# A hybrid attention encoder block: the product over wo's sums moved by two steps, and the switch of the output lag by eight

## The chip, the cores and the metric

The kernel runs on one core of one Trainium2 chip. A core has a tensor engine (PE, with its weight loads shown apart as PEld), a vector engine (DVE), a scalar engine (ACT), a GpSimd engine (POOL) and a sync engine (SP), which here issues all transfers. [...] The metric is device time in microseconds (us); lower is better.

## The reference

One encoder layer over x (1024 tokens, 1024 features, float32):

```python
h = einsum('bsd,de->bse', x, w_in)             # 21 blocks of 128 columns, and the values
q_a, k_a, v_a, z_a, q_b, k_b, v_b, z_b = split(h)
y_a = neighborhood_attention(q_a, k_a, v_a, rel_bias)     # 8 heads, 8x16 window on a 16x64 grid
y_b = windowed_gqa_with_sink(rotary(q_b), rotary(k_b), v_b, sink)   # 8 query heads, 2 key heads, |i-j| <= 128
mixed = concat([y_a * silu(z_a), y_b * silu(z_b)])
y = einsum('bse,ed->bsd', mixed, w_out)
x = layer_norm(alpha * x + y, gain, bias)
```

## The kernel before, in words

Every float32 operand of a product is split into two float16 tiles, a high and a low part, and each product becomes three 16-bit products (high by high, high by low, low by high) that add up in one PSUM bank. For that, weights are brought to a common power of two. For the output weights wo the power comes from sums of magnitudes: 16 blocks of wo are loaded and summed on ACT (L1025) or DVE (L1027) into the 16 columns of `wom`, and `wo_scale` (L796 to L805) makes the factors of them:

```python
ps = bank("t")
nc.tensor.matmul(ps[:, :16], ones, wom.bitcast(BF16)[:, 1::2], start=True, stop=True)   # L798
# L799 to L804: six DVE instructions on one column each, to wog, wos, wsn and yc
```

**Steps and units.** The attention is 128 units, first 64 of group b (SWA), then 64 of group a (NA): for each pair of heads p, each half j, eight blocks. The main loop goes through steps; step i issues unit i's scores (`stage_qk`, two matmuls, L890 and L891, into one of four PSUM banks "s", and a DVE instruction L904 that adds the bias and finds the row's extreme) and its exponential on ACT (L920). Unit i-1 is split in the same step (ACT L938, DVE L939) and handed to a transposing transfer that SP issues (L941). The bank of unit n is free for unit n+4 when L939 of unit n is done.

**Rounds and the lag.** Four units make a round q. Its product with the values (`stage_pv`, L967) takes one of two PSUM banks "t"; a step later DVE divides by the row sums (`stage_on`, L976 and L983), which frees that bank. Every second finished round of the right kind is turned back on PE (`stage_ot`, four transposes, L1005) into a "t" bank, and DVE multiplies it into z: in group b by four instructions L992, two in the round's first step and one each in the third and fourth, in group a by one instruction L1011. `stage_ot(q-1)` and `stage_pv(q)` stand in the first step of round q, and round and place in the round come from the step number:

```python
q, m = divmod(i - LP - 3 - (i < LATE), 4)      # L1502, LP = LPP = 6
```

So round q starts at step 4q + 10 while i < LATE, and at step 4q + 9 from then on. LATE is 4*22 + 6 + 7 = 101. Group b's even rounds have transposes; in group a it is rounds 4p + 19 and 4p + 20 (19 and 20, 23 and 24, 27 and 28).

**What fills PE.** Between the scores, a generator hands out the matmuls of 15 projections (L444, 48 each), so many to each step, and at the end of the loop the first products with wo (L1239). The rest of the output projection (a Strassen-like scheme over wo's blocks, with tiles T, m, A, wo) and the layer norm follow in `final`.

**The planner.** Work that is not tied to a step (splits of weights, sums of wo's blocks) is queued by engine with a priority, dependences on earlier pieces and a cost. At each step the planner books an engine's assumed time (`due`) against the assumed time of the step (`at_step`) and issues queued pieces where it finds room (`pop`, `fill_in`). All this happens while the program is written: on the chip the order is fixed. `t_prep(i)` queues, for one block row of wo: four differences (L1072, "any" engine), four high parts on ACT (L1077), four low parts (POOL L1065 and L1066, or DVE L1063) and four stores to DRAM by SP (L1080). They need `wsn`, so `t_prep` is called right behind `wo_scale`, together with four loads of the second block row (L1019), which wait for the low parts of the first.

**Where wo_scale stands.** At the top of a step, ahead of the step's scores and of `stage_ot` and `stage_pv`, under this condition:

```python
if i >= T_GO and i % 4 == 0 and len(scans) == 16 and all(op.step is not None and op.fin + 3 < at_step(i) for op in scans):
```

T_GO is 24. It holds first at step 44, the third step of round 8.

Of the kernel before, what the change touches and what calls it, by code (L numbers as in the profile page):

```python
# [27 lines left out]
LTT, LPP, BH, ND, NA, NX, F1 = 1, 6, 9, 1, 1, 8, 0.2  # L28
# [24 lines left out]
T_GO = 24  # L53
POOL_Q, DVE_ADD, DVE_OWN = 2, range(112, 124), 1.1
M2_AT, M3_AT = 113, 122
LATE = 4 * 22 + LPP + 7
WORK = {"act": 0.55, "dve": 0.63, "pool": 1.2}
STEP = (1.88, 1.5, 1.2)
ROOM = {"act": 0.35, "dve": 0.5, "pool": 0.0}
# [7 lines left out]
def hybrid_block(ctx, tc, xT, x, wt, wv, wo, bias, sink, gain, lbias, cos, sin, bmask, out):  # L67
# [116 lines left out]
    def at_step(i):  # L184
        return STEP[0] * i - (STEP[0] - STEP[1]) * max(0, i - 121) - (STEP[1] - STEP[2]) * max(0, i - 128)
# [610 lines left out]
    def wo_scale():  # L796
        ps = bank("t")
        nc.tensor.matmul(ps[:, :16], ones, wom.bitcast(BF16)[:, 1::2], start=True, stop=True)  # L798
        nc.vector.tensor_reduce(wog, ps[:, :16], axis=mybir.AxisListType.X, op=ALU.max)  # L799
        nc.vector.tensor_scalar_max(wog, wog, 2.0 ** -30)  # L800
        nc.vector.tensor_scalar(wog.bitcast(I32), wog.bitcast(I32), 0x7F800000, None, op0=ALU.bitwise_and)
        nc.vector.tensor_scalar(wos.bitcast(I32), wog.bitcast(I32), 0x7F800000, None, op0=ALU.bitwise_xor)
        nc.vector.tensor_scalar_mul(wsn, wos, 0.25)
        nc.vector.tensor_scalar(yc, wog, mc, 4.0, op0=ALU.mult, op1=ALU.mult)  # L804
        book("dve", 0.9)  # L805
# [6 lines left out]
    def gather_v(p):  # L812
        t = va[p] = big_ap([128, 8, 4 * VE], F16, f"va{p}")
        bulk["last"] = bulk["step"]
        nc.sync.dma_start(t, vd[p].rearrange("(k c) r e -> (c r) k e", k=8))
# [40 lines left out]
    def stage_load(u, i):  # L856
        g, p, j, t = u
        if g == "a" and t == 0:
            bulk["last"] = clock["step"] + 1
            bt = big_ap([128, BWIN[3]], F32, "bias")  # L860
            nc.sync.dma_start(bt, bias[2 * p + j])
            ld = Op("sp", None, [], 1)
            ld.step = i
            op = enq("pool", lambda: nc.gpsimd.tensor_scalar(bt, bt, rsg, -1.0, op0=ALU.mult, op1=ALU.mult),
                     ld, prio=0)
            st["bias", p, j] = bt, op
# [77 lines left out]
    def quad(q):  # L944
        g, p, j, t = units[4 * q]
        return g, p, j, t // 4
# [38 lines left out]
    def stage_z(n):  # L985
        for _ in range(n if st.get("z") else 0):
            ps, k, h, e, m = st["z"].pop(0)
            o = ps.rearrange("p (b h c) -> p b h c", h=2, c=64)
            r = slice(64 * e, 64 * e + 64)
            z = zt[k][r, 512 * h:512 * h + 512].rearrange("p (b m c) -> p b m c", m=2, c=64)[:, :, m]  # L990
            book("dve", 0.42)
            nc.vector.scalar_tensor_tensor(z, o[64 * m:64 * m + 64, :, e], z_col(k)[r], z, op0=ALU.mult, op1=ALU.mult)  # L992
# [23 lines left out]
    scans = []  # L1016

    def wo_load(i, b, *deps):
        load_ops["wor", i, b] = enq("sp", lambda: nc.sync.dma_start(wor[:, b], wo[i, :, b]), *deps)  # L1019

    def wo_scan(i, b):
        def scan(eng):
            m = wom[:, 4 * i + b:4 * i + b + 1]
            if eng == "act":
                nc.scalar.activation(junk2, wor[:, b], AF.Abs, accum_out=m)  # L1025
            else:
                nc.vector.tensor_reduce(m, wor[:, b], axis=mybir.AxisListType.X, op=ALU.add, apply_absolute_value=True)  # L1027

        scans.append(enq("any", scan, load_ops["wor", i, b], prio=1.9,
                         cost={"act": 0.85, "dve": 0.68} if (clock["step"] or 0) > 4 else {"act": 0.85}))  # L1030
# [62 lines left out]
    def t_soon(n):  # L1093
        def load():
            t = big_tile(f"T{n}", (128, 2, 2, 512), F16)
            nc.sync.dma_start(t.rearrange("p i h c -> p i (h c)"), td[:2, :, n].rearrange("i p c -> p i c"))
            pair_of(t, *[(("T1", "T3", "T4", "T2")[n], i) for i in range(2)])

        load_ops["T", n] = enq("sp", load, *t_ops)
# [3 lines left out]
    def x_soon(t):  # L1103
        def load():
            xr_[t] = big_tile(f"xr{t}", (128, D), F32)
            nc.sync.dma_start(xr_[t], x[t])

        enq("sp", load)

    def b_load(n, *deps):  # L1110
        key, i = B_KEYS[n]
        b = ("B11", "B12", "B21", "B22").index(key)

        def load():
            b_raw[n] = wp.tile([128, 512], F32, tag="wr", name=f"wob{n}", bufs=5)
            nc.sync.dma_start(b_raw[n], wo[i, :, b])

        load_ops["wo", n] = enq("sp", load, *deps)
# [325 lines left out]
    for i in range(-LD, NU + LO):  # L1444
        if 0 <= i + LD < NU:
            stage_load(units[i + LD], i)
        if i < 0:
            continue
        clock["step"] = i
        per, h = divmod(i, 16)  # L1450
        bulk["step"] = i
        if (i - LP - 3 - (i < LATE)) % 4 > 1:
            stage_z(1)
        if i == VA_AT:
            gather_v(0)
        if i in SCAN_LD:
            n, b = divmod(NSCAN + SCAN_LD.index(i), 4)
            wo_load(SCAN[n], b, *scans[-4:-3])
            wo_scan(SCAN[n], b)
        if i >= T_GO and i % 4 == 0 and len(scans) == 16 and all(op.step is not None and op.fin + 3 < at_step(i) for op in scans):  # L1460
            wo_scale()
            scans.clear()
            t_prep(0)
            for b in range(4):
                wo_load(1, b, t_low[(0, 1, 3, 2)[b]])
            t_prep(1)
        if i in B_LD:
            n = B_LD.index(i)
            b_load(n, w_ops[NL - 5 + n] if n < 5 else b_ops[n - 5])
        if i in B_AT:  # L1470
            b_split(B_AT.index(i))
        if i in M_AT:
            m_queue(M_AT.index(i))
        if i == M2_AT:
            m_kq(2, ("A11", "A12", "A21", "A22"))
        if i == M3_AT:
            m_kq(3, ("A11", "A21"))
        if i == 129:
            t_soon(0)
            x_soon(0)  # L1480
            t_soon(3)
            x_soon(4)
            x_soon(1)
            t_soon(1)
            t_soon(2)
        if bulk["last"] == i:
            sp_at.append(i)
        if i >= 118:
            pop("sp", 3)
        elif sum(j > i - 3 for j in sp_at) < 2:  # L1490
            kept = len(queues["sp"])
            pop("sp", 1)
            if len(queues["sp"]) < kept:
                sp_at.append(i)
        if i < NU:
            u = units[i]
            if u[0] == "b" and u[3] == 0:
                need(*[o for j in range(2) for o in stk_ops[f"b{u[1]}", j, u[2]]])
            if u[0] == "a" and u[3] == 0:
                need(*stk_ops[u[1], u[2], 0], *stk_ops[u[1], u[2], 1])  # L1500
            stage_qk(u)
        q, m = divmod(i - LP - 3 - (i < LATE), 4)  # L1502
        if i >= Q30 + 2:
            q, m = (NU // 4 - 2, i - Q30 - 2) if i < Q30 + 4 else divmod(i - LP - 3, 4)
        elif i >= Q30:
            q, m = -1, 0
        if m == 0 and 0 <= q - 1 < NU // 4:
            stage_ot(q - 1)
        if m == 0 and 0 <= q < NU // 4:
            stage_pv(q)  # L1510
        kept = len(queues["dve"])
        pop("dve", 2, 0)
        if m > 1 and len(queues["dve"]) == kept and i not in DVE_ADD and i < DVE_ADD[-1] and due["dve"] + DVE_OWN < at_step(i + 1):
            fill_in("dve")
        if 0 <= i - LT < NU:
            stage_tr(units[i - LT])
        pop("act", 1, 0)
        pump_to(i + F1)
        if 0 <= q < NU // 4:
            g, p, j, h = quad(q)  # L1520
            if g == "a" and p < 3 and (j, h, m) == VA_STEP:
                gather_v(p + 1)
        if m == 1 and 0 <= q < NU // 4:
            stage_on(q)
        pop("dve", ND, same=True)
        if i < NU:
            stage_exp(units[i])
        held = [op.prio for op in queues["act"] if op.prio <= 1]
        pop("act", NA if 0 in held or i < 105 and len(held) < 5 else 2)
        pop("pool", NP)  # L1530
        for eng in ("pool", "act", "dve")[:3 if i in DVE_ADD or len(scans) and i <= T_GO + 8 else 2]:
            for _ in range(2):
                if free_at(eng, ROOM[eng]):
                    fill_in(eng)
        pump_to(i + 1)
# [78 lines left out]
```

## Time and profile before

| | us |
|---|---|
| median of 3 runs | 440.12 (439.98 to 440.93) |
| the profiled execution's own time | 439.81 |
| its span, first to last instruction | 438.0 |
| PE busy in the span | 431.2 |
| DVE, ACT, POOL busy | 338.6, 308.8, 276.2 |

The page's first part gives each engine's busy time. A matmul's end in it is modelled and matmuls overlap, so for PE the distance from start to start tells more than the duration. In a timeline a row is a start, a length, an engine, a line of the kernel, the operation with the tiles it writes and reads, and a count where rows of one kind are merged; in brackets stands how long the engine had been idle and what ended that. In the waits view a row says who waited for whom, for how long in total, how many times, and the longest.

### The profile page before, as it was taken

What the parts mean: (1) busy time and instruction counts of PE and PEld (TensorE: products, weight loads), DVE (VectorE), ACT (ScalarE), POOL (GpSimd) and SP (SyncE); (2) the same over time, 40 slices, a digit from 0 to 9 for tenths busy, and PEclk for the clock granted to TensorE, in tenths of its full rate; (3) what the DMA queues carried; (4) which work ended last, traced back from release to release, by engine and by line L of the source; (5) the groups of instructions that cost most, each with busy time, mean ns of one, the idle gap of its engine ahead of it and who ended that gap; (6) DMA issues with size and microseconds to landing.
All of it is one profiled execution on the core that took longest, in us unless ns stands there. A gap on an engine that the chain in (4) does not pass through costs nothing.

```text
span 438.0 us, 9413 instructions
## 1 busy us (share of the span) xinstructions
PE 431.2 (98%) x3225; PEld 253.1 (58%) x3225; DVE 338.6 (77%) x854; ACT 308.8 (71%) x663; POOL 276.2 (63%) x295
## 2 busy tenths in 40 slices
PE   9999999999999999998999999999999999999996
PEld 8997754444455656554556555565656555444445
DVE  5978976785877788888898898879887855675456
ACT  4849789768688978788888869887978753322321
POOL 0110074578438648779988799898899931058585
PEclk9999999999999999999999999999999999999999
DMA  7922379994329999897879999997989669811113
GB/s 253 406 102 61 125 236 331 260 299 161 118 62 192 218 179 197 162 182 147 171 153 203 187 217 186 228 203 141 187 201 236 128 123 334 338 48 73 73 73 121
DMA packets 128817, 80.10 MB, mean 183 GB/s; under 512 B 97280, under 2 KB 106368, under 8 KB 128768
## 3 DMA queue, kind: packets, MB, share of 16 engines
q1 hardware_dynamic: 128624, 79.36, 74.3%
q8 instruction: 25, 0.41, 0.4%
q14 instruction: 24, 0.20, 0.2%
q10 hardware_dynamic: 144, 0.13, 0.1%
HBM read 47.97 MB, written 8.42 MB: 129 GB/s over the span
## 4 chain that ended last, share of the span: by engine, by line
PE 73%; DVE 9%; ACT 7%; issue 6%; POOL 3%; DMA 1%; DVEq 0%; SPq 0%; ACTq 0%; POOLq 0%
PE ps_pj L444 35%; PE ps_s L1239 8%; PE ps_s L551 6%; PE ps_t L967 5%; PE ps_pj L1239 4%; PE ps_pj L551 3%; PE ps_t L551 3%; PE ps_s L890 2%; PE ps_s L891 2%; PE ps_t L1239 2%; DVE split L939 2%; DVE sn L904 2%; ACT ps_s L920 2%; POOL xr L1348 2%; POOL xr L1349 2%
## 5 line engine op out<-in xcount | busy, mean ns | idle before, releaser
L444 PE MATMUL ps_pj<-xf,wh 128*128 128x512 f16 x672 | 201.3, 379 | 0.0
L444 PE MATMUL ps_pj<-xf,wl 128*128 128x512 f16 x336 | 127.3, 379 | 0.0
L444 PEld LDWEIGHTS <-wh 128*128 128x128 f16 x672 | 63.8, 98 | 58.2
L920 ACT ACTIVATE ps_s<-sn,nm 128x321 f32<-128x321 f32 (+3 forms) x128 | 67.7, 529 | 35.8 <-DVE nm L904 34.5
L939 DVE SCALAR_TENSOR_TENSOR split<-ps_s,split 128x320 f16<-128x320 f32 (+2 forms) x128 | 62.8, 490 | 16.3 <-ACT split L938 14.9
L247 POOL TENSOR_SCALAR wr<-wr,wsc 128x512 f32<-128x512 f32 x32 | 22.9, 716 | 67.5 <-ACT wh L242 64.9
L938 ACT ACTIVATE split<-ps_s 128x320 f16<-128x320 f32 (+2 forms) x128 | 55.1, 430 | 1.7
L444 PEld LDWEIGHTS <-wl 128*128 128x128 f16 x336 | 32.9, 98 | 37.8
L248 POOL TENSOR_TENSOR wl<-wr,wh 128x512 f16<-128x512 f32 x32 | 40.2, 1257 | 2.7
L904 DVE CUSTOM_DVE_ANT_0 sn<-ps_s,bias,sg 128x368 f32<-128x368 f32 (+1 forms) x64 | 36.2, 565 | 5.8 <-PE ps_s L891 5.3
L904 DVE CUSTOM_DVE_ANT_0 sn<-ps_s,bm,nsk 128x320 f32<-128x320 f32 (+2 forms) x64 | 36.8, 575 | 4.7 <-PE ps_s L891 4.2
L890 PE MATMUL ps_s<-ks,qs 128*128 128x320 f16 (+3 forms) x128 | 38.2, 298 | 0.1
L891 PE MATMUL ps_s<-ks,qs 128*128 128x320 f16 (+3 forms) x128 | 38.2, 298 | 0.0
L967 PEld LDWEIGHTS <-tr 128*128 128x128 f16 (+1 forms) x1056 | 36.2, 98 | 1.7
L1239 PEld LDWEIGHTS <-m 128*128 128x128 f16 x198 | 19.0, 98 | 20.9 <-issue 0.2
L361 POOL COPY ks<-ks 64x512 f16<-64x512 f16 x40 | 26.3, 658 | 3.6 <-ACT ks L305 0.7
L1274 DVE SCALAR_TENSOR_TENSOR xr<-ps_s,yc,xr 128x512 f32<-128x512 f32 (+1 forms) x22 | 15.8, 724 | 13.9 <-PE ps_s L1239 13.5
L1346 ACT ACTIVATE xr<-xr,nmr,rstd 128x1024 f32<-128x1024 f32 x6 | 7.4, 1240 | 27.0 <-POOL nmr L1293 27.0
L1239 PEld LDWEIGHTS <-A 128*128 128x128 f16 x162 | 15.2, 98 | 15.7
L551 PEld LDWEIGHTS <-xf 128*128 128x128 f16 x192 | 18.6, 98 | 7.2
L242 ACT ACTIVATE wh<-wr,wsc 128x512 f16<-128x512 f32 x32 | 22.7, 710 | 0.0
L1348 POOL TENSOR_TENSOR xr<-xr,gb 128x512 f32<-128x512 f32 x13 | 16.9, 1302 | 8.1 <-ACT xr L1346 8.1
(223 smaller groups left out, 909.9 us busy)
## 6 DMA issues: line engine op xcount, KB each, us to landing
wr<-in_wt SPq DMA_DIRECT2D x32, 256.0 KB, 3.5
ws<-in_wt SPq DMA_DIRECT2D x15, 512.0 KB, 7.0
wor<-in_wo SPq DMA_DIRECT2D x20, 256.0 KB, 4.0
xr<-in_x SPq DMA_DIRECT2D x8, 512.0 KB, 10.3
out<-xr SPq DMA_DIRECT2D x15, 256.0 KB, 2.0
wob<-in_wo SPq DMA_DIRECT2D x14, 256.0 KB, 3.9
bias<-in_bias SPq DMA_DIRECT2D x8, 440.0 KB, 4.6
wvraw<-in_wv SPq DMA_DIRECT2D x9, 320.0 KB, 5.6
```

The source lines that it names most:

```text
L248: nc.gpsimd.tensor_sub(l, raw, h)
L361: nc.gpsimd.tensor_copy(place(t, o, half, col), place(t, a, half, col))
L444: nc.tensor.matmul(ps, a[:, k % 4, :], mv, start=(k == 0 and i == 0), stop=(k == KT - 1 and i == 2))
L551: nc.tensor.matmul(ps[:, :320], lh[:, ts], rh[:, cs], start=(k == ko[0] and i == 0), stop=(k == ko[-1] and i == 2))
L890: nc.tensor.matmul(ps[:, :n], q, sl[0], start=True, stop=False)
L891: nc.tensor.matmul(ps[:, :n], q, sl[1], start=False, stop=True)
L904: nc.vector.tensor_tensor_reduce(sn[:, at0:at0 + n], ps[:, :n], bias_t, sg[:, c:c + 1], init, op0=ALU.add, op1=ALU.min, accum_out=nm)
L920: nc.scalar.activation(pt[:, c], sn[:, c], AF.Exp, bias=nm, scale=-1.0, accum_out=acc)
L938: nc.scalar.activation(h, pt[:, c], AF.Copy, scale=PSCALE)
L939: nc.vector.scalar_tensor_tensor(l, pt[:, c], PSCALE, h, op0=ALU.mult, op1=ALU.subtract)
L967: nc.tensor.matmul(ps[:, w * m:w * m + e], a, b_, start=(i == 0), stop=(i == len(mms) - 1))
L1239: nc.tensor.matmul(ps[:, cs], lh[:, 128 * t:128 * t + 128], rh[:, cs], start=(fresh and e == 0 and n == 0), stop=(e == len(terms) - 1 and ...
```

## The change

Two constants of the schedule change:

```diff
-LATE = 4 * 22 + LPP + 7
+LATE = 4 * 24 + LPP + 7
...
-        if i >= T_GO and i % 4 == 0 and len(scans) == 16 and all(op.step is not None and op.fin + 3 < at_step(i) for op in scans):
+        if i >= T_GO and i % 8 == 6 and len(scans) == 16 and all(op.step is not None and op.fin + 3 < at_step(i) for op in scans):
             wo_scale()
             scans.clear()
             t_prep(0)
```

The first makes LATE 109: rounds 23 and 24 start at steps 102 and 106 instead of 101 and 105; all rounds before and behind them stay. The round that loses its fourth step is then round 24 instead of round 22. The second makes `wo_scale`, and with it `t_prep(0)`, the four loads and `t_prep(1)`, stand at the top of step 46, the first step of round 9, which has no transposes. No instruction is added or removed by name; which engine takes a queued piece, and when, is for the planner to decide anew.

## The prediction

> **What bounds the kernel now.** I read the page's first part, then the busy time of stretches, then who made PE wait, then the timelines around those waits. The page:
>
> ```profile
> span 438.0 us, 9413 instructions
> PE 431.2 (98%) x3225; PEld 253.1 (58%) x3225; DVE 338.6 (77%) x854; ACT 308.8 (71%) x663; POOL 276.2 (63%) x295
> ```
>
> Two of the stretches (bounds, length, busy time by engine, granted PE clock, DMA share, GB/s), and the waits of PE:
>
> ```profile
> 199.20:200.60 1.40, 0.10 (x3) 0.07 (x3) 1.32 (x6) 1.34 (x4) 1.32 (x2) 1.00 0.69 156
> 200.60:306.00 105.40, 105.31 (x942) 60.82 (x942) 91.35 (x258) 86.36 (x196) 93.88 (x100) 1.00 0.92 184
> ```
>
> ```profile
> PE ps_t L798 <- DVE on L983: 1.3, 1, 1.3
> PE ps_t L477 <- DVE warm L133: 1.0, 1, 1.0
> PE ps_t L1313 <- DMA out<-xr: 0.5, 1, 0.5
> PE ps_t L1005 <- DVE on L983: 0.4, 1, 0.4
> ```
>
> PE works at the full clock almost without a hole. Of its four listed waits one lies in the start-up (L477) and one in the tail (L1313); the other two are the product that moves (L798) and the transposes at the head of a round (L1005). So the kernel is bound by PE's own work, and the holes between start-up and tail are at the two places that the change touches.
>
> **Part 1, the product: what it costs now.**
>
> ```profile
> 198.42 0.59 PE L444 MATMUL ps_pj<-xf,wh 128*128 128x512 f16 x2
> 198.85 0.38 PE L444 MATMUL ps_pj<-xf,wl 128*128 128x512 f16 x1
> 200.53 0.18 PE L798 MATMUL ps_t<-wom,ones 128*128 128x16 bf16 x1 [1.30 <-DVE on L983]
> 200.57 0.30 PE L890 MATMUL ps_s<-ks,qs 128*128 128x320 f16 x1
> ```
>
> ```profile
> 203.70 0.27 PE L890 MATMUL ps_s<-ks,qs 128*128 128x256 f16 x1
> ...
> 203.92 0.25 PE L967 MATMUL ps_t<-vb,tr 128*128 128x64 f16 x3
> ```
>
> Two matmuls of 512 columns take 198.85 - 198.42 = 0.43 us from start to start, one 0.21. From 198.85 to 200.53 are 1.68, so PE stood for 1.68 - 0.21 = 1.47 us. The product itself costs 200.57 - 200.53 = 0.04. What DVE did then:
>
> ```profile
> 200.05 0.42 DVE L983 TENSOR_TENSOR on<-ps_t,ri 128x256 f32<-128x256 f32 x1
> 200.51 0.48 DVE L992 SCALAR_TENSOR_TENSOR z<-ps_t,zc,z 64x256 f32<-64x256 f32 x1
> ...
> 201.98 0.60 DVE L904 CUSTOM_DVE_ANT_0 sn<-ps_s,bm,nsk 128x320 f32<-128x320 f32 x1
> ...
> 203.03 0.49 DVE L992 SCALAR_TENSOR_TENSOR z<-ps_t,zc,z 64x256 f32<-64x256 f32 x1
> ```
>
> In step 44 both "t" banks are in use: one holds round 8's product until L983 ends at 200.47, the other holds transposes until the fourth L992 (203.03, step 45). The product got the first of them, and PE's whole queue stood behind it.
>
> **Part 1, the new place.** At the top of step 46 the bank of L983 is long free. PE reached step 46's scores at 203.70 and L967 at 203.92; without the hole and the 0.04 it reaches the product at 202.19, and L967, with the 0.04 paid there, at 202.45. The other "t" bank comes free with the fourth L992. DVE's six small instructions (L799 to L804, between L992's end at 200.99 and 201.98: 0.99 us) leave step 44 too, so that the fourth L992 ends near 203.52 - 0.99 = 202.53. Either L967 needs that bank, a wait of some 0.1 us, or the product does, 0.34. A gain it cannot be, since nothing waits now at that place. I take 0.1, since in step 44 the bank that came free first was given out; ends 0 and 0.4. The six DVE instructions run in step 46 instead and are covered if DVE has time to spare there, the next point.
>
> **Does the rest follow PE?** PE can be early only if DVE and ACT free its score banks earlier as well. From 200.6 to 214.5 DVE waited for PE, and ACT for DVE:
>
> ```profile
> DVE sn L904 <- PE ps_s L891: 2.1, 3, 1.0
> ```
>
> ```profile
> 214.88 0.53 ACT L920 ACTIVATE ps_s<-sn,nm 128x321 f32<-128x321 f32 x1 [1.20 <-DVE nm L904]
> ```
>
> DVE has 2.1 us to give before step 51 is over, and 1.47 are needed; ACT has these 1.2 and what it stood before. So at 214 both can be 1.47 us earlier. Behind that PE's margins are thin:
>
> ```profile
> 253.04 0.54 DVE L939 SCALAR_TENSOR_TENSOR split<-ps_s,split 128x368 f16<-128x368 f32 x1
> ```
>
> ```profile
> 268.87 0.54 DVE L939 SCALAR_TENSOR_TENSOR split<-ps_s,split 128x368 f16<-128x368 f32 x1
> ```
>
> ```profile
> 254.05 0.32 PE L890 MATMUL ps_s<-ks,qs 128*128 128x368 f16 x1
> ```
>
> ```profile
> 268.99 0.38 PE L444 MATMUL ps_pj<-xf,wl 128*128 128x512 f16 x1
> 269.46 0.32 PE L890 MATMUL ps_s<-ks,qs 128*128 128x368 f16 x1
> ```
>
> L939 frees the bank for L890 of the unit four further on: 0.47 us ahead (253.58 to 254.05), and at 269.46 PE stands for it, 0.47 - 0.21 = 0.26 us. That small hole I leave as it is. If DVE, ACT and PE all move by 1.47, the margins stay.
>
> **Part 1, what else moves.** `t_prep(0)` queues four differences, four high and four low parts and four stores; then come four loads and a second set, all two steps (2 x 1.57 = 3.1 us, 200.57 to 203.70) later. On POOL the four L1072 come about 3 us later, but POOL stands longer than that a little on (226 to 240, then 240 to 255):
>
> ```profile
> POOL wr L247 <- ACT wh L242: 1.4, 1, 1.4
> POOL bias L864 <- DMA bias<-in_bias: 0.8, 1, 0.8
> ```
>
> ```profile
> POOL bias L864 <- DMA bias<-in_bias: 2.0, 1, 2.0
> ```
>
> 4.2 us in which it catches up. ACT's pieces (shortest, median and longest in ns, first and last start)
>
> ```profile
> L1077 ACT ACTIVATE wohl<-wor,wsn x8: 705/707/722, 217.6 to 294.5; 128x512 f16<-128x512 f32 x8
> ```
>
> are moved along a chain whose margin for PE is 0.47 or less: one more of them ahead of a thin place costs up to 0.7, one fewer gives back the hole of 0.26. I take 0, with ends of -0.3 and +0.7. On SP, stores and loads stand between the transposing transfers; a store that waits for POOL holds the transposes behind it, in 200 to 260 for
>
> ```profile
> SPq L1080 <- POOL m L1173: 0.5, 1, 0.5
> SPq L1080 <- POOL wohl L1066: 0.2, 1, 0.2
> ```
>
> at most 0.5 us. I take 0; this is where a loss would come from (below). The pieces are used in the output projection; the last of POOL's splits that its first part needs waited for ACT, so POOL had no backlog there:
>
> ```profile
> 350.50 1.16 POOL L1173 TENSOR_TENSOR m<-z,m 128x512 f16<-128x512 f32 x1 [0.40 <-ACT m L1170]
> ```
>
> ```profile
> 355.06 0.81 PE L1239 MATMUL ps_pj<-wo,m 128*128 128x512 f16 x3
> ```
>
> From 351.66 to 355.06 are 3.4 us, so PE may be 1.9 us earlier without meeting it.
>
> **Part 2, the longer lag.** The switch at step 101 puts the transposes of round 23 two steps behind L983 of round 22 instead of three:
>
> ```profile
> 305.79 0.32 PE L891 MATMUL ps_s<-ks,qs 128*128 128x368 f16 x1
> 306.48 0.63 PE L1005 MATMUL ps_t<-identf,on 128*128 128x128 f32 x4 [0.37 <-DVE on L983]
> ```
>
> ```profile
> 277.07 0.32 PE L891 MATMUL ps_s<-ks,qs 128*128 128x368 f16 x1
> 277.22 0.60 PE L1005 MATMUL ps_t<-identf,on 128*128 128x128 f32 x4
> ```
>
> 306.48 - 305.79 = 0.69, against 277.22 - 277.07 = 0.15 where nothing is waited for: 0.54 us. With the switch at 109 the transposes stand behind the next step's scores, a step's matmuls (1.57 us) later than what PE had reached at 305.94, and so 1.2 us behind L983's end at about 306.3: the wait is gone. Round 25, behind the new switch, has no transposes, and the "t" bank that it takes was freed three steps before: 0 there. Rounds 23 and 24 read their transposed tiles a step later; those tiles' buffers come free a step later for SP's transfers of the rounds behind, as in all rounds before, in which PE went without a hole. L983 and L1011 of the two rounds move by a step on DVE, and step 101 gains a place where the planner may give DVE a queued piece; both lie beside PE. I take -0.54, with ends of 0 and -0.54.
>
> **The tail** is a chain of DVE, ACT and POOL work that PE's last products start; it moves with PE.
>
> **Sum.** -1.47 + 0.1 - 0.54 = -1.91 us; the ends are -1.47 - 0.54 - 0.3 = -2.3 and -1.47 + 0.4 + 0.7 = -0.4. Against the profiled 439.81: 437.90, span 436.1. That execution was 0.31 below the median, so against 440.12: 438.2.
>
> [...]
>
> **The rivals.**
> - *The hole comes back at 269.* If DVE and ACT do not arrive earlier (the six instructions in step 46 and new pieces eat the 2.1 us), PE waits for them at 254 and 269, and part 1 gives nothing: 440.12 - 0.54 = 439.6. For it: margins of 0.47 and 0. Against: 2.1 exceeds 1.47.
> - *Slower: SP held by a store.* `t_prep`'s stores are placed by the planner's times; on the chip POOL is 3 us later at this place. A store that waits for it holds the transposes, and PE's L967 with them. It decides where the holds cost PE 1.9 us beyond what the lag covers; a hold of 3 us that no lag covers, 1.1 beyond that point, gives 440.12 - 1.9 + 3 = 441.2. For it: stores waited already. Against: by 0.5 at most, and they move together with what they wait for.
> - *The change doesn't do what it says.* The product takes the other bank, and round 25 waits as round 23 did: 1.47 - 0.4 = 1.07 less, 439.05. Against: round 25 has no transposes.
>
> **How the numbers follow.** The forecast 0.70, with a range of its own from 437.5 to 438.9; the hole at 269 0.13; the third rival 0.07; slower 0.10. Faster by over 0.2% (0.9 us, about what a measurement can tell from no change here) takes the forecast, the third rival and a part of the first: 0.80. Within 0.2%: 0.11. Slower: 0.09. The range of 8 in 10 goes from 437.4 to 440.0.
>
> **What would show it.** Right: no wait of L798 or L1005 for L983, PE busy for about 431 in a span near 436, at most 0.4 us lost at step 46. Wrong: new holes of PE ahead of L890 between 214 and 300 with DVE L939 as releaser, or ahead of L967 with a transfer as releaser, or SP waiting for POOL by microseconds.

## The result, and the profile after

| | before | after |
|---|---|---|
| median of 20 runs, measured side by side, us | 440.15 | 438.77 |
| after by before, with its 95% interval | | 0.9963 (0.9946 to 0.998) |
| the profiled execution's own time | 439.81 | 438.85 |
| its span | 438.0 | 437.0 |

The ratio makes 440.15 x 0.0037 = 1.6 us (0.9 to 2.4). Measured once more beside other kernels, the changed kernel took 438.54, at 0.9971 (0.995 to 0.9993) of the kernel before. So it is faster, by about 0.3%, and 0.6 us slower than the 438.2 forecast. Of the profiled span only 1.0 us went, where the sum had 1.9. The page of the changed kernel, and the waits of PE in it (who waited for whom, us in total, times, longest):

```profile
span 437.0 us, 9409 instructions
PE 431.1 (99%) x3225; PEld 253.3 (58%) x3225; DVE 337.6 (77%) x855; ACT 308.3 (71%) x663; POOL 275.6 (63%) x293
```

```profile
PE ps_t L477 <- DVE warm L133: 1.0, 1, 1.0
PE ps_t L1313 <- DMA out<-xr: 0.5, 1, 0.5
PE ps_t L967 <- DVE z L992: 0.2, 1, 0.2
PE ps_s L890 <- DVE split L939: 0.2, 1, 0.2
```

L798 and L1005 are gone from the list, and two waits are new in it. The places, in the timeline of PE after the change (start, length, engine, line, tiles, idle time and what ended it), and what DVE did beside the first of them:

```profile
202.30 0.17 PE L798 MATMUL ps_t<-wom,ones 128*128 128x16 bf16 x1
202.33 0.27 PE L890 MATMUL ps_s<-ks,qs 128*128 128x256 f16 x1
202.44 0.27 PE L891 MATMUL ps_s<-ks,qs 128*128 128x256 f16 x1
202.95 1.21 PE L967 MATMUL ps_t<-vb,tr 128*128 128x64 f16 x36 [0.24 <-DVE z L992]
...
268.01 0.38 PE L444 MATMUL ps_pj<-xf,wl 128*128 128x512 f16 x1
268.61 0.32 PE L890 MATMUL ps_s<-ks,qs 128*128 128x368 f16 x1 [0.22 <-DVE split L939]
...
306.54 0.32 PE L891 MATMUL ps_s<-ks,qs 128*128 128x368 f16 x1
306.70 0.60 PE L1005 MATMUL ps_t<-identf,on 128*128 128x128 f32 x4
```

```profile
200.38 0.43 DVE L983 TENSOR_TENSOR on<-ps_t,ri 128x256 f32<-128x256 f32 x1
200.83 0.48 DVE L992 SCALAR_TENSOR_TENSOR z<-ps_t,zc,z 64x256 f32<-64x256 f32 x1
...
202.40 0.49 DVE L992 SCALAR_TENSOR_TENSOR z<-ps_t,zc,z 64x256 f32<-64x256 f32 x1
```

- The product waits for nothing: it takes the bank that L983 freed at 200.81. The rest of step 46 pays for that. L967 gets the other bank, which the fourth L992 frees at 202.89, and starts at 202.95. Without a wait it would follow L891 by 0.11, as L891 follows L890: 0.51 - 0.11 = 0.40 us.
- L890 of step 82 waits for L939: 0.60 from the start of L444, where 0.22 is usual: 0.38 us, and 0.26 before.
- L1005 follows L891 by 0.16: its 0.53 us are gone, and nothing waits at the new switch.

So in the loop PE wins 1.47 + 0.53 and loses 0.40 + 0.12: 1.48. By the first scores of unit 0 and of unit 127 the loop is 233.79 long before (121.91 to 355.70) and 232.29 after (122.01 to 354.30), 1.50 less; the start-up was 0.10 later in this execution. The tail keeps its length, 79.34 from unit 127's first score down to the issue of the last transfer, the only one that ACT issues and not SP. Its row in the timeline of before:

```profile
435.04 0.37 ACTq L1322 DMA_DIRECT2D out<-xr  x1
```

and in that of after, 1.40 earlier:

```profile
433.64 0.37 ACTq L1322 DMA_DIRECT2D out<-xr  x1
```

The ends of the two spans are less than 1.40 apart: 2.95 us behind that row before, 3.40 behind it after (to the hundredth, where the page has 438.0 and 437.0). 0.45 us are lost where no program work is left, and this was in no term of the forecast. The experiments go after the two surprises: whether the loss at step 46 comes back later, and what makes the end longer.

### The profile page after: what moved, and what is told of

Same layout as the page of the kernel before. It is cut to its first block, busy times and chain, and to the rows that moved or that the text cites. A ratio compares the mean times of both kernels' runs of the same rounds, so it can differ in the third digit from the quotient of the medians.

```text
span 437.0 us, 9409 instructions
## 1 busy us (share of the span) xinstructions
PE 431.1 (99%) x3225; PEld 253.3 (58%) x3225; DVE 337.6 (77%) x855; ACT 308.3 (71%) x663; POOL 275.6 (63%) x293
## 4 chain that ended last, share of the span: by engine, by line
PE 79%; DVE 6%; ACT 6%; issue 4%; POOL 3%; DMA 1%; SPq 0%; DVEq 0%; ACTq 0%; POOLq 0%
PE ps_pj L444 39%; PE ps_s L1239 8%; PE ps_s L551 6%; PE ps_t L967 6%; PE ps_pj L1239 4%; PE ps_pj L551 3%; PE ps_t L551 3%; PE ps_s L890 3%; PE ps_s L891 3%; PE ps_t L1239 2%; POOL xr L1348 2%; POOL xr L1349 2%; DVE split L939 1%; ACT ps_s L920 1%; PE ps_t L1005 1%
## 5 line engine op out<-in xcount | busy, mean ns | idle before, releaser
L444 PE MATMUL ps_pj<-xf,wh 128*128 128x512 f16 x672 | 201.3, 379 | 0.0
L444 PE MATMUL ps_pj<-xf,wl 128*128 128x512 f16 x336 | 127.3, 379 | 0.0
L444 PEld LDWEIGHTS <-wh 128*128 128x128 f16 x672 | 63.7, 98 | 58.3
L939 DVE SCALAR_TENSOR_TENSOR split<-ps_s,split 128x320 f16<-128x320 f32 (+2 forms) x128 | 62.7, 490 | 19.6 <-ACT split L938 18.3
L938 ACT ACTIVATE split<-ps_s 128x320 f16<-128x320 f32 (+2 forms) x128 | 55.1, 430 | 1.7
L444 PEld LDWEIGHTS <-wl 128*128 128x128 f16 x336 | 32.8, 98 | 37.8
L890 PE MATMUL ps_s<-ks,qs 128*128 128x320 f16 (+3 forms) x128 | 38.2, 298 | 0.2 <-DVE split L939 0.2
L891 PE MATMUL ps_s<-ks,qs 128*128 128x320 f16 (+3 forms) x128 | 38.2, 298 | 0.0
L967 PEld LDWEIGHTS <-tr 128*128 128x128 f16 (+1 forms) x1056 | 36.2, 98 | 2.1 <-issue 0.4
```

Source lines behind the costliest of these rows:

```text
L444: nc.tensor.matmul(ps, a[:, k % 4, :], mv, start=(k == 0 and i == 0), stop=(k == KT - 1 and i == 2))
L890: nc.tensor.matmul(ps[:, :n], q, sl[0], start=True, stop=False)
L891: nc.tensor.matmul(ps[:, :n], q, sl[1], start=False, stop=True)
L938: nc.scalar.activation(h, pt[:, c], AF.Copy, scale=PSCALE)
L939: nc.vector.scalar_tensor_tensor(l, pt[:, c], PSCALE, h, op0=ALU.mult, op1=ALU.subtract)
L967: nc.tensor.matmul(ps[:, w * m:w * m + e], a, b_, start=(i == 0), stop=(i == len(mms) - 1))
```

## Experiments

Diffs are against the changed kernel. The loop is the distance from the first score of unit 0 to that of unit 127; a hole is the distance from start to start less the usual one; the end is the distance from the last transfer's issue to the end of the span. All are from each run's timeline; the hole at L798 is 1.46 with the usual distance taken as 0.216, 1.47 by the rounded rows. Beside the experiments the kernel before took 439.73 to 439.84. A ratio is not exactly the quotient of two medians, and where medians were taken at different times, the ratios are what to compare.

| kernel | median | ratio (95%) | loop | holes at L798, L967 of step 46, L890 of step 82, L1005 of step 101 | end |
|---|---|---|---|---|---|
| before | 440.15 | 1 | 233.79 | 1.46, 0, 0.26, 0.53 | 2.95 |
| after | 438.77 | 0.9963 (0.9946 to 0.998) | 232.29 | 0, 0.40, 0.38, 0 | 3.40 |
| after again | 438.54 | 0.9971 (0.995 to 0.9993) | 232.31 | 0, 0.45, 0.34, 0 | 3.41 |
| product alone | 438.68 | 0.9985 (0.9971 to 0.9999) | 233.22 | 0, 0.68, 0.37, 0.64 | 2.95 |
| lag alone | 440.23 | 1.0024 (1.0007 to 1.004) | 233.38 | 1.62, 0, 0.23, 0 | 3.40 |
| product in step 47 | 438.76 | 0.9979 (0.9965 to 0.9993) | 231.75 | 0, 0, 0.23, 0 | 3.40 |
| score bank, step 44 | 438.98 | 0.9978 (0.996 to 0.9995) | 232.66 | 0, 0, 0.59, 0 | 3.39 |
| step 47, old lag | 438.14 | 0.9967 (0.9946 to 0.9988) | 232.23 | 0, 0, 0.27, 0.43 | 2.97 |
| after, 5 on POOL | 438.42 | 0.9971 (0.9948 to 0.9994) | 232.49 | 0, 0.60, 0.38, 0 | 2.97 |
| step 47, 5 on POOL, 3 on DVE | 438.13 | 0.9963 (0.9939 to 0.9988) | 231.77 | 0, 0, 0.25, 0 | 2.96 |
| that, no ACT piece in 77, 78 | 438.34 | 0.9969 (0.9951 to 0.9987) | 231.52 | 0, 0, 0, 0 | 2.96 |
| that, no ACT piece in 77 to 80 | 439.44 | 1.0001 (0.9981 to 1.0021) | 233.58 | 0, 0, 0.10, 0 | 3.32 |

The first score itself started between 121.40 and 122.73 in these executions, in part since start-up waits come and go (PE's L268 for ACT's L262, 0.3 to 0.6 us in four of the twelve). That is as much as most of the differences looked for, so each mechanism is read from its rows and the total only bears it out or not.

**Each part alone.**

```diff
-LATE = 4 * 24 + LPP + 7
+LATE = 4 * 22 + LPP + 7
```

> The product in step 46, the lag's switch left at step 101. If the two parts add up: PE's 1.47 us at L798 are gone, L967 of step 46 waits 0.40 as in the changed kernel, L890 at 269 waits 0.26 to 0.38, and L1005 at step 101 stands for its 0.54 as before; PE's last score is 1.47 - 0.40 - 0.12 = 0.95 us earlier than before, 440.15 - 0.95 = 439.2. The rival, that part 1 gives nothing because PE meets DVE again at 269: a hole of about 1.3 there and no gain, 440.15.

```diff
-        if i >= T_GO and i % 8 == 6 and len(scans) == 16 and all(
+        if i >= T_GO and i % 4 == 0 and len(scans) == 16 and all(
```

> The lag's switch at step 109, the product left in step 44. If the two parts add up: L798 stands for 1.47 us as before, L1005 at the old switch waits no more and nothing waits at step 109; PE's last score is 0.54 us earlier, 440.15 - 0.54 = 439.6. The rival, that the wait only moves to the new switch: a hole of about 0.5 at step 109 and no gain, 440.15.

The product alone:

```profile
201.70 0.17 PE L798 MATMUL ps_t<-wom,ones 128*128 128x16 bf16 x1
201.73 0.27 PE L890 MATMUL ps_s<-ks,qs 128*128 128x256 f16 x1
201.83 0.27 PE L891 MATMUL ps_s<-ks,qs 128*128 128x256 f16 x1
202.62 0.45 PE L967 MATMUL ps_t<-vb,tr 128*128 128x64 f16 x10 [0.52 <-DVE z L992]
...
304.59 0.32 PE L891 MATMUL ps_s<-ks,qs 128*128 128x368 f16 x1
305.39 0.30 PE L1005 MATMUL ps_t<-identf,on 128*128 128x128 f32 x1 [0.48 <-DVE on L983]
```

Its holes stand where they were expected, but L967's is 0.68 instead of 0.40 and L1005's 0.64 instead of 0.54. At L967, PE was early, ready at 201.94, while the fourth L992 ended at 202.57. The loop is 0.57 shorter where 0.95 was expected; the ratio (0.66 us) agrees, and the rival (nothing gained) is excluded.

The lag alone missed its 439.6. Its mechanism came as expected (no hole at L1005 and none at step 109, loop 0.41 shorter), and yet it is slower than the kernel before: its end is 0.45 longer, and so is a piece of the tail, which its timeline shows:

```profile
431.14 0.29 DVE L1280 BATCH_NORM_STATS2 stats<-xr 128x6 f32<-128x128 f32 x1
431.91 0.37 DVE L1284 BATCH_NORM_AGGREGATE mv<-stats 128x2 f32<-128x48 f32 x1 [0.47 <-POOL xr L1299]
```

In the kernel before these two rows are:

```profile
431.47 0.29 DVE L1280 BATCH_NORM_STATS2 stats<-xr 128x6 f32<-128x128 f32 x1
431.87 0.37 DVE L1284 BATCH_NORM_AGGREGATE mv<-stats 128x2 f32<-128x48 f32 x1
```

L1284 follows L1280 by 0.77 instead of 0.40, so PE's first L1313 comes 0.37 later than in the kernel before, counted from unit 127. Together 0.45 + 0.37 = 0.82, twice what PE won in the loop.

**Another place, another bank.** The product one step later, and the product back in step 44 with a score bank:

```diff
-        if i >= T_GO and i % 8 == 6 and len(scans) == 16 and all(
+        if i >= T_GO and i % 8 == 7 and len(scans) == 16 and all(
```

> As the changed kernel, but the product alone one step later, in step 47 (DVE's six small instructions follow it; ACT, POOL and SP keep their order). Theory: L967 waited 0.40 us at step 46 because the product ahead of it had taken the bank that was already free; now L967 gets that bank, the product gets the other, free since the fourth L992, and neither waits. PE is 0.40 us earlier and keeps it: 438.77 - 0.40 = 438.4, with the hole at 269 unchanged near 0.38. Rival: DVE is back to back from 200 to 214 and sets when L939 frees the banks, so PE loses the same 0.40 again: a hole of about 0.78 at 269, 438.8.

```diff
     def wo_scale():
-        ps = bank("t")
+        ps = bank("s")
...
-        if i >= T_GO and i % 8 == 6 and len(scans) == 16 and all(
+        if i >= T_GO and i % 4 == 0 and len(scans) == 16 and all(
```

> As the changed kernel, but the product back in step 44 and into one of the four score banks instead of a t bank. Theory, that the hole at step 44 was the t bank alone and not the product's place: no hole at L798 and no wait of L967 at step 46; the differences of wo's blocks come two steps earlier, in the order of the kernel before, and the hole at 269 goes back to 0.26: 440.15 - 1.47 - 0.54 = 438.15. Rival: with one score bank used up by the product, the scores of steps 44 to 46 stand behind an L939 that is one unit nearer and PE waits up to 1 us there: 439.1.

In step 47 neither the product nor L967 waits. That execution alone does not prove it, since PE came so late (L967 at 202.88) that the fourth L992 was done (202.51). The same place with the old lag does, below. The hole at step 82 did not grow by the 0.40; it shrank to 0.23. So DVE's chain does follow PE, and the rival of a DVE that takes everything back falls. The total did not show the 0.40: it is 438.76, where 438.4 was expected and the rival said 438.8. This program has the 0.77 at L1284 that the changed kernel has not, which takes 0.37 back, and the same 3.40 at the end.

With the score bank, PE's timeline at the old place and DVE's fourth L992 are:

```profile
198.99 0.38 PE L444 MATMUL ps_pj<-xf,wl 128*128 128x512 f16 x1
199.20 0.17 PE L798 MATMUL ps_s<-wom,ones 128*128 128x16 bf16 x1
199.23 0.30 PE L890 MATMUL ps_s<-ks,qs 128*128 128x320 f16 x1
...
202.58 0.40 PE L967 MATMUL ps_t<-vb,tr 128*128 128x64 f16 x8
```

```profile
203.40 0.49 DVE L992 SCALAR_TENSOR_TENSOR z<-ps_t,zc,z 64x256 f32<-64x256 f32 x1
```

The product stands in step 44 and costs 0.03: the 1.47 of the kernel before were the bank alone, not the place. L967 starts 0.82 ahead of the fourth L992, in the bank of L983. No L890 of steps 44 to 46 waits, so the rival is wrong. The hole at step 82 (0.59) did not go back to 0.26 although wo's pieces stand in the old order again: that part of the theory is wrong. That PE is ahead doesn't explain it alone: with the product in step 47, unit 81's first score stands 144.21 behind unit 0's, here 144.77, and the hole is smaller there (0.23 to 0.27). Why it is 0.59 here stays open. There is also one of 0.40 at 178.35, ahead of any difference in PE's, DVE's or ACT's order, which I put down to the execution. The total, 438.98, missed the expected 438.15 and came near the rival's 439.1 for other reasons: besides these two holes the program has the 0.77 at L1284 and 3.39 at the end.

**The product in step 47 with the old lag, and what the end is made of.** The next four ran beside each other:

> The changed kernel once more, beside the next three. All theories: L967's wait of 0.3 to 0.7 at step 46, no wait of L798 or L1005, and 2.8 to 3.5 us from the issue of the last transfer (L1322) to the end of the span. If the 3.36 us of that stretch (2.96 in the kernel before) is a property of the program it is 3.3 to 3.5 again; if it scatters from execution to execution it can be either.

```diff
-LATE = 4 * 24 + LPP + 7
+LATE = 4 * 22 + LPP + 7
...
-        if i >= T_GO and i % 8 == 6 and len(scans) == 16 and all(
+        if i >= T_GO and i % 8 == 7 and len(scans) == 16 and all(
```

> The product in step 47, the lag's switch left at step 101. Theory, that the longer lag gives PE 0.5 us and takes back as much or more behind the loop: PE's holes are 0.2 to 0.4 at 269 and 0.53 to 0.64 at L1005, so its last score is about 1.4 to 1.6 earlier than before; L1322 to the end of the span takes 2.96 as before; 440.0 - 1.5 = 438.5, no slower than the same product place with the longer lag (438.76). Rival, that the longer lag is worth its 0.54 in the total: 0.54 slower than that, 439.3.

```diff
+    pad = const.tile([128, 16], F32, name="pad")
...
+        if 100 <= i < 105:
+            nc.gpsimd.memset(pad[:, i - 100:i - 99], 0.0)
```

> The changed kernel with five memsets of one column added to POOL's queue, one each in steps 100 to 104; nothing reads them. [...]

The last has `i % 8 == 7`, the lines above and these:

```diff
+        if 100 <= i < 103:
+            nc.vector.memset(pad[:, i - 92:i - 91], 0.0)
```

> The product in step 47, the longer lag, the five memsets on POOL and three of one column on DVE (steps 100 to 102). [...] The kernel with the product in step 47 took 438.76; less 0.37 and 0.4 makes 438.0. Rival, that L1284's wait is for POOL's L1299, as the waits say: it stays, and the time is 438.4.

Step 47 with the old lag, PE and then DVE:

```profile
202.30 1.21 PE L967 MATMUL ps_t<-vb,tr 128*128 128x64 f16 x36
...
204.64 0.17 PE L798 MATMUL ps_t<-wom,ones 128*128 128x16 bf16 x1
204.67 0.24 PE L890 MATMUL ps_s<-ks,qs 128*128 128x192 f16 x1
```

```profile
202.46 0.49 DVE L992 SCALAR_TENSOR_TENSOR z<-ps_t,zc,z 64x256 f32<-64x256 f32 x1
```

L967 starts before the fourth L992 does. It has L983's bank, and the wait at step 46 was made by the product's standing ahead of it. The expected 438.5 came as 438.14: with the shorter lag, the kernel keeps a hole of 0.43 at L1005 and is not clearly slower than any with the longer one. So the longer lag gives PE about what the forecast said (loops of 231.75 and 232.23) and here no time. With the product in step 46 it did better: the ratio is 0.9985 without it and 0.9963 with it, with intervals that overlap a little. L1284 doesn't stand in that pair, and 0.28 of the difference in the loop is L967's wait, which scatters.

Now the end. The view of L1610, the program's last line, counts by instruction (shortest, median and longest in ns, first and last start); the first pair is from before, the second from after:

```profile
L1610 POOLq DRAIN  x3: 34/78/1054, 432.3 to 437.7; - x3
...
L1610 POOLq EVENT_SEMAPHORE_RANGE_CLEAR  x1: 96/96/96, 437.6 to 437.6; - x1
```

```profile
L1610 POOLq DRAIN  x3: 77/182/1052, 430.9 to 436.6; - x3
...
L1610 POOLq EVENT_SEMAPHORE_RANGE_CLEAR  x1: 96/96/96, 436.2 to 436.2; - x1
```

Between the clearing of the semaphores and the last DRAIN, POOL goes on at once before and stands for 0.3 us after. The second execution of the changed kernel has an end of 3.41, so it is the program's. The trace of before holds 461 instructions of POOL, waits included, that of after 455: two fewer that work (295 and 293 on the pages; one low part, L1065 and L1066, became DVE's L1063) and four fewer waits. In all twelve traces POOL's 453rd instruction is the point: with 455, 457 or 458 in all it is among the last six, behind POOL's wait for SP, and the end takes 3.32 to 3.41; with 459 to 461 it is that wait or comes ahead of it, and the end takes 2.95 to 2.97. In the six traces with the long end three different instructions stand there (the last DRAIN, the DRAIN ahead of the clearing, a semaphore instruction), each 0.32 to 0.37 us behind the end of the one before it, where 0.03 to 0.07 is usual. Five memsets that nothing reads make 455 into 460. The transfers from 434 to 440 (queue, kind: packets, MB, share), of the changed kernel:

```profile
q10 hardware_dynamic: 144, 0.13, 6.2%
q14 instruction: 1, 0.01, 0.4%
```

and the last issue with the memsets, one line further down in that kernel:

```profile
core 0 of [0], span 436.4 us
...
433.44 0.37 ACTq L1323 DMA_DIRECT2D out<-xr  x1
```

The end is 2.97 again, and no instruction packet moves in that stretch. L1284 behaves alike in part: 0.77 in the three kernels whose trace has 1097 instructions of DVE, where it is the 1088th, and 0.40 in all others (1094 to 1096, and 1100 with the three memsets):

```profile
429.97 0.29 DVE L1281 BATCH_NORM_STATS2 stats<-xr 128x6 f32<-128x128 f32 x1
430.37 0.37 DVE L1285 BATCH_NORM_AGGREGATE mv<-stats 128x2 f32<-128x48 f32 x1
```

So the waits view named POOL's L1299 as its releaser without cause: in the kernel before, L1284 starts at 431.87 and L1299 ends only at 432.07. One thing does not fit a fixed position on DVE as it stands: in the six traces with 1094 to 1096 instructions the 1088th is one of L1315 to L1317, which starts at most 0.04 us behind the end of the one before it, and nothing is lost. Why L1284 stands at that place and these don't isn't shown. In the totals the 0.4 to 0.8 us are at the edge of what can be told: 438.42 against 438.54 beside it with POOL's five, 0.12 less where the end is 0.44 shorter, and 438.13 with both and step 47, where 438.0 was expected (0.37 is L1284's 0.77 less 0.40, 0.4 the end's 3.40 less 2.97) and the rival said 438.4.

**The hole at step 82.** ACT gets no queued piece in two, then in four steps (on the kernel with both paddings):

```diff
-                if free_at(eng, ROOM[eng]):
+                if free_at(eng, ROOM[eng]) and (eng != "act" or i not in (77, 78)):
```

> The kernel with the product in step 47 and the memsets, and ACT is given no queued piece in steps 77 and 78: the piece L1125 that ran there (0.71 us, between the exponential of unit 78 and the copies of ks that DVE waited 0.6 for) goes behind unit 80. Theory, that the hole of 0.25 at step 82 is made by ACT's pieces ahead of it, which make DVE and its L939 late: the hole shrinks or goes, PE's last score is up to 0.25 earlier, 437.9. Rival, that DVE's own work sets it: the hole stays at 0.25 and the time at 438.1.

> The same with ACT given no queued piece in steps 77 to 80, so that two pieces L1125 and one L1077 (2.1 us of ACT) go behind unit 82. Theory: no hole at step 82, PE's last score 0.25 earlier, 437.9, unless the pieces open another one behind step 82. Rival, that DVE's own work sets it: the hole stays at 0.25 and the time at 438.1.

With two steps the waits of PE are these:

```profile
PE ps_t L478 <- DVE warm L134: 1.0, 1, 1.0
PE ps_t L269 <- ACT junk L263: 0.6, 1, 0.6
PE ps_t L1314 <- DMA out<-xr: 0.5, 1, 0.5
PE ps_pj L552 <- ACT wvh L508: 0.4, 1, 0.4
```

None lies in the loop: it is the only one of the twelve with no hole, and the shortest, 231.52. Moving one piece of 0.71 us on ACT by two steps removes the hole. The rows show the way: without this edit DVE's L939 at 264.73 waits 0.41 for ACT's L938, which stands behind the piece; with it, the same instruction, at 264.71, waits for nothing, although PE is 0.48 later in this execution. The total (438.34) doesn't show these 0.25; the first score of that execution, at 122.73, was the latest of all. With four steps 0.10 of the hole is left and the pieces pile up behind step 82: holes of 0.33 (L1005), 0.24 (L890) and 0.33 (L1005) at 277 to 285, and POOL comes to 458 instructions, with 3.32 at the end. A hole of 0.74 at 186, ahead of the edit, adds to the 440.0 of the profiled execution; whether the others, with their median of 439.44, had it isn't known.

## Why the prediction came out as it did

- **Direction, range and time: right.** 438.77 and 438.54 lie in the forecast's own range of 437.5 to 438.9, towards its slow end. The sum of 1.91 was too large.
- **Part 1, the hole at L798, -1.47: right**, to a hundredth; with a score bank in the same step it vanishes as well, so its cause (the bank) is shown, too.
- **Part 1, the new place, +0.1: right in kind, wrong in size.** L967 waits for the fourth L992, by 0.40, 0.45, 0.60 and 0.68 in the four traces with the product ahead of it. The term was the difference of two estimated times, PE at 202.45 and L992's end at 202.53. PE came at 201.94 to 202.55 and L992 ended at 202.57 to 202.89. Each scatters by more than the 0.1 that I took. The choice of bank was right, the size was not: 0.40 to 0.68 stands where 0.1 was taken, and the sign that the forecast set itself, at most 0.4 us lost at step 46, held in the first of the four alone.
- **DVE and ACT follow PE: right.** The loop is shorter by what the holes say, to 0.02. The hole at step 82 that I left as it is grew by 0.12, and it is not fixed: 0.34 to 0.38 with the product in step 46, 0.23 to 0.27 in step 47 or with a t bank in step 44, 0.59 with the score bank, and none where one ACT piece is moved. The first rival falls: 0.38 is not 1.3.
- **What else moves, 0 each: right.** The second rival did not come: after the change, the waits of SP from 200 to 262 hold one row of a store that waits for POOL,

```profile
SPq L1080 <- POOL wr L247: 0.3, 1, 0.3
```

- **Part 2, -0.54: right for PE, wrong for the total.** Of the edit's ends (0 and -0.54) none allowed a loss, and the lag alone loses. The failing step is "both lie beside PE" with "the tail moves with PE": with the planner's new choices POOL has 455 instructions instead of 461 (457 with the lag alone, 459 and no longer end with the product alone), its 453rd falls into the end, and that costs 0.45 there. I had costed the moved instructions and not how many each engine has.
- **The balance of the profiled spans.** 1.91 forecast; less 0.30 (bank), 0.12 (step 82), 0.45 (end) and 0.10 (start-up) is 0.94, and the spans differ by 0.95.
- **The third rival did not come either:** the product takes the bank that is first free, and nothing waits at step 109.

A matmul's row is longer than PE's pace: the rows of L444 last 0.38 and start 0.22 apart (medians of the profile before). So the idle figures of the two new waits (0.24 and 0.22) are well below the distances of starts (0.40 and 0.38); by the idle figures the loop would have won 1.30 + 0.37 - 0.24 - 0.22 = 1.21, by the starts 1.48, and it won 1.50.

## What to carry to other kernels

Before a small operation is moved away from a bank that it waits for, look at who takes the next bank of that kind: the wait may only pass to the matmuls behind it (here 0.40 to 0.68 us of it did), and here a place behind them, or a bank of another pool, removed it. When a planner lays out the queues anew, compare the totals of instructions on each engine, and look at the stretch between the last transfer and the end of the span: here five memsets that nothing reads took 0.44 us from it (3.41 to 2.97). Where the executions scatter by as much as the effect, the mechanism is settled by rows, and the totals only limit it.

## What the runs showed of the hardware

In six of the twelve traces POOL stands for 0.32 to 0.37 us ahead of its 453rd recorded instruction, and the end takes 3.32 to 3.41, against 2.95 to 2.97 in the other six. In three, DVE stands ahead of its 1088th (L1284 0.77 behind L1280 against 0.40). Where that place fell on the engine's wait for another one, or ahead of it, no time was lost: POOL with 459 to 461 instructions (the end of 2.95 to 2.97), DVE with the three memsets (the 0.40). In the six traces with 1094 to 1096 instructions of DVE it cost nothing either (the 1088th starts at most 0.04 us behind the end of the one before it), though DVE waited for no other engine there. The profile's page gives the transfers of instructions, after the change:

```profile
q8 instruction: 25, 0.41, 0.4%
q14 instruction: 23, 0.19, 0.1%
```

0.19 MB in 23 packets are some 8 KB each, 0.41 MB in 25 some 16 KB. In the six traces with the long end a packet of 8 KB starts 0.70 to 0.72 us behind the start of POOL's 453rd instruction (after the change at 437.35, against 436.63), and in the six others none starts in the end. What the engine stands for isn't shown: these packets start only behind the stall, and no row says what the engine waits for.
